# A hybrid SSD/GLA layer on one core: the first block's sums of squares taken from the columns of x by TensorE, columns in eight buffers, the first unit's split weights stored in block two

## The chip, the cores and the metric

The kernel runs on one core of one Trainium2 chip. The metric is device time in microseconds (us) of one execution. A core has five engines that run their own instruction streams and wait for each other by semaphores: PE (TensorE, matrix products; its weight loads are listed apart as PEld), DVE (VectorE), ACT (ScalarE), POOL (GpSimd) and SP (SyncE, which here only issues DMA transfers). "DVEq", "SPq" and so on are the instruction queues of the engines. Data lives in the chip's main memory (HBM) and is brought by DMA into the on-chip buffer (SBUF); PE writes its results into accumulation banks (PSUM).

## The reference

One layer of a decoder. 16 learned "meta" tokens are put in front of 2048 tokens of width 1024; each token is normalised by its root mean square; one combined projection gives the inputs of two branches and their gates:

```python
h = concatenate([meta_tokens, x], axis=1)              # (1, 2064, 1024)
u = h * rsqrt(mean(h * h, axis=-1) + EPS) * norm_w     # rmsnorm
proj = einsum('bld,dn->bln', u, w_in)
z, xbc, dt_raw, q, k, v, g_gla, a_lr, merge_g = split_cols(proj, IN_WIDTHS)
...
branches = stack([y_ssd, y_gla], axis=2)
merged = sum(sigmoid(merge_g) * einsum('blnc,ncd->blnd', branches, w_branch), axis=2)
out = rmsnorm(h + einsum('bld,de->ble', merged, w_out))[:, N_META:]
```

`y_ssd` comes from a causal convolution and a Mamba-2 scan, `y_gla` from gated linear attention; both carry a state from chunk to chunk. The change touches only how u is formed for the first tokens, and when some split weights are stored.

## The kernel before, in words

**Blocks and units.** The 2048 tokens are worked on in four blocks of 512 (four chunks of 128); the first block has the 16 meta tokens in front, 528 columns in all. In each block eight units run in a fixed order: four of the SSD branch (`ssd_proj`, i = 0 to 3) and four of the GLA branch (`gla_proj`). A unit projects u with its weights on PE; the scans that follow are generators, of which `step()` runs a piece at each `yield` of the unit. For PE and SP the order of the program is the order of execution (`manual_schedule`); on the other engines, and for the start ahead of the blocks, a scheduler orders by program order among what is ready in its own simulation. After the four blocks a second part computes gates, branch products and output.

**Split precision.** u and the weights are split in two parts each, hi = rounded to the matrix format by ACT, lo = value - hi; a product is three matmuls (`accum`, L176 to L179: hi x hi at L177, hi x lo at L178, lo x hi at L179).

**Weights.** `load_w` (L155) gives a split weight tile. The first time a key is seen, in block one, it loads the raw tile into one of three `wr` buffers (L163), ACT copies it to hi (L164), POOL subtracts to lo (L165) into one of four `whl` buffers, and the pair is put on a list to be stored in HBM as `k_...`; `save(n)` (L170 to L173) issues those stores on SP until n are left, and is called with 2 before each raw load and with 0 at the end of each block. In the later blocks a tile comes back already split, by one DMA (L159). The very first unit has the key `zm`: eight tiles of 128 x 288 (one for each 128 rows of the weight), used in pairs; for each pair four chunks of 128 tokens, and in block one the meta tokens, are multiplied (`proj_tok`). It yields once, before its third pair.

**The side job.** In block two, from unit 0 on, `beside_unit` forms sums of pieces of `w_out`: `make_sums` takes two of the three `wr` buffers, loads four pieces on SP (L76), subtracts on POOL (L80), and stores by the ACT queue (L83). It takes its first step at the yield in the middle of unit zm.

**u for a block.** `load_u(b)` (L229): for each chunk the rows of x are read, ACT squares and sums them (L241), and r = (mean + eps)^-0.5 follows on DVE and POOL (L250, L251). PE spreads r over the partitions by a matmul with the identity (L264, L268). Then for each of eight column tiles `xk` (128 features x 528 tokens, from `xmt`, the transposed x) DVE multiplies by norm_w and r (L280), ACT makes uh (L282), the ACT queue stores the tile as `u_left` (L283), and DVE makes ul (L284). `xk` uses the tag `acc`, which has two buffers. For the first block all of it runs ahead of the first unit; for the others it runs beside unit 4 of the block before.

Of the kernel before, what the change touches and what calls it, by code (L numbers as in the profile page):

```python
# [19 lines left out]
NCH = BLK // P  # L20
# [3 lines left out]
EPS = 1e-6  # L24
NWR = 3
NSQ = 5
NT4 = 5
NACT = 8
# [12 lines left out]
def trunk_kernel(ctx: ExitStack, tc: tile.TileContext, xm, xmt, w_feat, w_tok, w_zm, w_br, w_o,  # L41
                 cf32, cmsk, pvec, fnw, hvec, gw2, out):
    nc = tc.nc
# [5 lines left out]
    def mk(pool, shape, dt, tag, **kw):  # L49
        cnt[0] += 1  # L50
        return pool.tile(shape, dt, tag=tag, name=f"{tag}_{cnt[0]}", **kw)

    base = ctx.enter_context(tc.tile_pool(name="base", bufs=1))
    wdram = ctx.enter_context(tc.tile_pool(name="wdram", bufs=1, space=bass.MemoryType.DRAM))
    dpool = ctx.enter_context(tc.tile_pool(name="dpool", bufs=2, space=bass.MemoryType.DRAM))
    mhalf = base.tile([P, 4], F32, name="mhalf")
# [3 lines left out]
    def left(name):  # L60
        return wdram.tile([P, BLK], F32, tag=name, name=name, bufs=1)

    u_left = [[left(f"u_{b}_{kt}") for kt in range(KT)] for b in range(nblk)]
# [40 lines left out]
    for s in range(nsb):  # L104
        b = 2 * s + 2
# [9 lines left out]
    upool = first.enter_context(tc.tile_pool(name="upool", bufs=2))  # L115
    wpool = first.enter_context(tc.tile_pool(name="wpool", bufs=3))
    bpool = first.enter_context(tc.tile_pool(name="bpool", bufs=1))
    wk = first.enter_context(tc.tile_pool(name="wk", bufs=2))
    sm = first.enter_context(tc.tile_pool(name="sm", bufs=4))
    const = first.enter_context(tc.tile_pool(name="const", bufs=1))  # L120
    pj = first.enter_context(tc.tile_pool(name="pj", bufs=3, space=bass.MemoryType.PSUM))
    pt = first.enter_context(tc.tile_pool(name="pt", bufs=3, space=bass.MemoryType.PSUM))
    pc = first.enter_context(tc.tile_pool(name="pc", bufs=2, space=bass.MemoryType.PSUM))

    def bank(pool, tag):
        return mk(pool, [P, 512], F32, tag)


    cst = const.tile([P, 4, P], F32, name="cst")
    ident = cst[:, 0, :]  # L130
    tri = cst[:, 1, :]
    tris = cst[:, 2:4, :]
    pv = const.tile([P, 118], F32, name="pv")
    norm_w = pv[:, 0:8]
# [7 lines left out]
    ones = ones_r.bitcast(F32)  # L142
# [9 lines left out]

    kept, unsaved = {}, []

    def load_w(key, src):  # L155
        n = src.shape[-1]
        hl = mk(wpool, [P, 2, 512], F32R, "whl", bufs=4)[:, :, :n]
        if key in kept:
            nc.sync.dma_start(hl.bitcast(F32), kept[key])  # L159
        else:  # L160
            save(2)
            raw = mk(wpool, [P, 512], F32, "wr", bufs=NWR)[:, :n]
            nc.sync.dma_start(raw, src)  # L163
            nc.scalar.activation(hl[:, 0], raw, AF.Copy)  # L164
            nc.gpsimd.tensor_tensor(hl[:, 1], raw, hl[:, 0].bitcast(F32), op=ALU.subtract)  # L165
            kept[key] = wdram.tile([P, 2, n], F32, tag="k_" + key, name="k_" + key, bufs=1)
            unsaved.append((kept[key], hl.bitcast(F32)))
        return hl[:, 0], hl[:, 1]

    def save(n):  # L170

        while len(unsaved) > n:
            nc.sync.dma_start(*unsaved.pop(0))  # L173
# [7 lines left out]
    def proj_feat(key, src, segs, moving):  # L181

        pss = [bank(pj, "pj") for _ in segs]
        for half in range(2):
            h, lo = load_w(f"{key}_{half}", src[:, half * 512:(half + 1) * 512])
            for k4 in range(4):
                kt = half * 4 + k4
                cs = slice(k4 * P, (k4 + 1) * P)
                for ps, (a, n) in zip(pss, segs):
                    accum(ps[:, :n], (h[:, cs], lo[:, cs]), moving(kt, a, n), kt == 0, kt == KT - 1)  # L190
        return pss

    def proj_tok(key, src, u, starts, banks, width=256, per=2, sub=None):

        nq = KT // per
        opened = set()
        for q0 in range(0, nq, 2):
            if q0 == nq // 2:  # L200
                yield
            ws = [load_w(f"{key}_{q}", src[:, q * per * width:(q + 1) * per * width]) for q in (q0, q0 + 1)]
            for i, ((bk, ps), a) in enumerate(zip(banks, starts)):
                c0 = sub if sub is not None and i >= NCH else 0
                for k2 in range(2 * per):
                    kt = q0 * per + k2
                    h, lo = ws[k2 // per]
                    cs = slice(k2 % per * width + c0, (k2 % per + 1) * width)
                    accum(ps[:, c0:width], tuple(t[:, kt, a:a + P] for t in u),
                          (h[:, cs], lo[:, cs]), bk not in opened, kt == KT - 1, skip_group_check=True)  # L210
                    opened.add(bk)
# [14 lines left out]
        nc.vector.tensor_tensor(lo, src, h.bitcast(F32), op=ALU.subtract)  # L226


    def load_u(b):  # L229
        m0 = META if b == 0 else 0  # L230
        row0 = META - m0 + b * BLK
        tt = m0 + BLK
        pair = mk(upool, [P, 2, KT * (META + BLK)], F32R, "u")[:, :, :KT * tt]
        uh, ul = [pair[:, i].rearrange("p (k t) -> p k t", k=KT) for i in range(2)]

        def rows_rstd(r0, n):
            ss = mk(sm, [P, 1], F32, "ss")
            if m0:
                xt = mk(wk, [P, D], F32, "tok4", bufs=NT4)
                nc.sync.dma_start(xt[:n], xm[r0:r0 + n, :])  # L240
                nc.scalar.activation(xt[:n], xt[:n], AF.Square, accum_out=ss[:n])  # L241
            else:
                s2 = mk(sm, [P, 2], F32, "ss2")
                for i in range(2):
                    xt = mk(wk, [P, META + BLK], F32, "acc")[:, :BLK]
                    nc.sync.dma_start(xt, xm[r0:r0 + n, i * BLK:(i + 1) * BLK])
                    nc.scalar.activation(xt, xt, AF.Square, accum_out=s2[:, i:i + 1])
                nc.vector.tensor_tensor(ss, s2[:, 0:1], s2[:, 1:2], op=ALU.add)
            r = mk(sm, [P, 1], F32, "rs1")
            nc.vector.tensor_scalar(r[:n], ss[:n], 1.0 / D, EPS, op0=ALU.mult, op1=ALU.add)  # L250
            nc.gpsimd.tensor_tensor(r[:n], r[:n], mhalf[:n, 0:1], op=ALU.pow)  # L251
            return r

        rs = []
        for c in range(NCH):
            rs.append(rows_rstd(META + b * BLK + c * P, P))
            yield
        if m0:
            rs.append(rows_rstd(0, META))
            nc.sync.dma_start(cst[:, :2], cf32[:, :2])  # L260
            nc.sync.dma_start(pv, pvec)
        rb = bank(pt, "pt")
        for c in range(NCH):
            nc.tensor.matmul(rb[:, c * P:(c + 1) * P], rs[c].to_broadcast([P, P]), ident, start=True, stop=True)  # L264
        rbs = [(rb, m0, BLK)]
        if m0:
            rm = bank(pt, "pt")
            nc.tensor.matmul(rm[:, :META], rs[NCH][:META].to_broadcast([META, P]), ident[:META, :META],  # L268
                             start=True, stop=True)
            rbs = [(rm, 0, META)] + rbs  # L270
        else:
            rbc = mk(wk, [P, 3 + META + BLK], F32, "cin")[:, :BLK]
            nc.scalar.activation(rbc, rb, AF.Copy)
            rbs = [(rbc, 0, BLK)]
            yield
        for kt in range(KT):
            xk = mk(wk, [P, META + BLK], F32, "acc")[:, :tt]
            nc.sync.dma_start(xk, xmt[:, kt, row0:row0 + tt])
            for ps, a, n in rbs:
                nc.vector.scalar_tensor_tensor(xk[:, a:a + n], xk[:, a:a + n], norm_w[:, kt:kt + 1], ps[:, :n],  # L280
                                               op0=ALU.mult, op1=ALU.mult)
            nc.scalar.activation(uh[:, kt, :tt], xk, AF.Copy)  # L282
            nc.scalar.dma_start(u_left[b][kt], xk[:, m0:])  # L283
            nc.vector.tensor_tensor(ul[:, kt, :tt], xk, uh[:, kt, :tt].bitcast(F32), op=ALU.subtract)  # L284
            yield
        return uh, ul

    next_u = {}

    def fetch_u(b):  # L290
        next_u[b] = yield from load_u(b)

    for _ in fetch_u(0):
        pass


    nc.sync.dma_start(cst[:, 2:], cf32[:, 2:])
    hv = const.tile([P, 2, NH], F32, name="hv")
# [11 lines left out]
    nc.scalar.activation(nega, hv[:, 1], AF.Exp)  # L310
    nc.vector.tensor_scalar(nega, nega, -1.0, None, op0=ALU.mult)

    w2r = mk(wk, [P, META + BLK], F32, "act", bufs=NACT)[:48, :512]
    for i in range(3):
        nc.sync.dma_start(w2r[16 * i:16 * i + 16, :], gw2)
    w2 = const.tile([48, 512], F32R, name="w2")
# [700 lines left out]
    for si, st in enumerate(stages):  # L1017
        for q in range(28):
            p, j = PS[q // 4], q % 4
# [5 lines left out]
    i = 14  # L1025
# [102 lines left out]
```

## Time and profile before

| what | value |
|---|---|
| three runs | 2385.71, 2382.58, 2387.70 us |
| their median | 2385.71 us |
| profiled execution: span from the first to the last instruction | 2382.4 us |
| mean granted TensorE clock in it | 0.976 |
| bytes moved by DMA | 518.07 MB, 217 GB/s over the span |
| busy PE, DVE, ACT, POOL | 95%, 66%, 50%, 29% |

The profile is of one execution; its span is the time from the first to the last instruction, and the time of a run has a little around it. A group's row reads: line, engine, operation, tiles written <- read, shapes, count | busy us, mean ns of one | idle time of the engine just before, and what released it. A row of the timeline reads: start us, length us, engine, line, operation, tiles, count [idle before <- releaser]. "PEclk" is the clock that was granted to TensorE, as a share of the full one.

### The profile page before, as it was taken

To read this page: it belongs to the slowest core of one execution; us is meant where nothing else is said; L and a number is where in the kernel's file an instruction comes from. 1 tells how busy PE (TensorE), PEld (TensorE's weight loads), DVE (VectorE), ACT (ScalarE), POOL (GpSimd) and SP (SyncE) were. 2 spreads that over 40 slices of the span, in tenths; PEclk is the share of its full clock that TensorE was granted. 3 is DMA by queue.
4 is the path that set the end of the run, shared out by engine and by line. 5 is a ranking of instruction groups with operands and counts; after the bars stand their busy time and mean duration, and the time that the engine had idled before them with its cause. 6 is when DMAs were issued, how large, how long until landed. Compare 5 with 4: busy or idle time off the path is not lost. (4 is left out here: it accounts for less than half of the span.)

```text
span 2382.4 us, 36669 instructions
## 1 busy us (share of the span) xinstructions
PE 2264.0 (95%) x12641; PEld 1970.8 (83%) x12641; DVE 1571.8 (66%) x2889; ACT 1187.5 (50%) x2764; POOL 680.0 (29%) x681
## 2 busy tenths in 40 slices
PE   6899999999999999999999999789989999998998
PEld 6889989888889988888989889668877788877786
DVE  4676665676675676676666655764757855786976
ACT  4665655465544455544455534364634445553443
POOL 3343433122222122321122100324433454332431
PEclk8999999999999999999999999789999999999999
DMA  8665875667786676786666654364777965787652
GB/s 271 213 209 193 293 240 190 225 201 235 245 276 184 215 220 220 258 267 199 208 213 212 205 167 143 131 217 136 263 248 264 313 198 173 251 264 225 231 177 106
DMA packets 301547, 518.07 MB, mean 217 GB/s; under 512 B 27696, under 2 KB 143664, under 8 KB 301360
## 3 DMA queue, kind: packets, MB, share of 16 engines
q1 hardware_dynamic: 231856, 452.66, 58.2%
q10 hardware_dynamic: 69504, 63.06, 8.0%
q8 instruction: 99, 1.62, 0.3%
q14 instruction: 88, 0.72, 0.1%
HBM read 368.42 MB, written 147.19 MB: 216 GB/s over the span
## 5 line engine op out<-in xcount | busy, mean ns | idle before, releaser
L177 PE MATMUL pj<-u,whl 128*128 128x512 f32 (+1 forms) x1184 | 447.4, 378 | 9.3 <-ACT g_all L420 3.3
L179 PE MATMUL pj<-u,whl 128*128 128x512 f32 (+1 forms) x1184 | 431.5, 364 | 0.8 <-POOL whl L165 0.8
L178 PE MATMUL pj<-u,whl 128*128 128x512 f32 (+1 forms) x1184 | 430.9, 364 | 0.0
L177 PE MATMUL pj<-whl,u 128*128 128x256 f32 (+1 forms) x992 | 289.9, 292 | 8.7 <-ACT u L282 6.1
L179 PE MATMUL pj<-whl,u 128*128 128x256 f32 (+1 forms) x992 | 284.1, 286 | 1.3 <-DVE u L284 1.3
L177 PE MATMUL psa<-b,a 128*128 128x512 f32 x640 | 255.5, 404 | 30.8 <-ACT sn L913 20.6
L178 PE MATMUL pj<-whl,u 128*128 128x256 f32 (+1 forms) x992 | 283.8, 286 | 0.7 <-POOL whl L165 0.5
L177 PEld LDWEIGHTS pj<-u,whl 128*128 128x128 f32 x1184 | 225.7, 191 | 47.1 <-ACT g_all L420 3.7
L179 PE MATMUL psa<-b,a 128*128 128x512 f32 x640 | 255.8, 400 | 2.3 <-DVE a L897 2.2
L179 PEld LDWEIGHTS pj<-u,whl 128*128 128x128 f32 x1184 | 225.2, 190 | 36.7 <-POOL whl L165 1.1
L178 PE MATMUL psa<-b,a 128*128 128x512 f32 x640 | 255.5, 399 | 0.0
L178 PEld LDWEIGHTS pj<-u,whl 128*128 128x128 f32 x1184 | 225.8, 191 | 33.2
L876 DVE TENSOR_TENSOR b<-br,b 128x512 fp32r<-128x512 f32 x196 | 160.8, 842 | 59.3 <-ACT b L875 58.9
L177 PEld LDWEIGHTS pj<-whl,u 128*128 128x128 f32 x992 | 191.0, 193 | 9.7 <-ACT u L282 6.6
L179 PEld LDWEIGHTS pj<-whl,u 128*128 128x128 f32 x992 | 191.2, 193 | 2.1 <-DVE u L284 2.1
L178 PEld LDWEIGHTS pj<-whl,u 128*128 128x128 f32 x992 | 191.1, 193 | 2.0 <-POOL whl L165 1.6
L897 DVE TENSOR_TENSOR a<-ar,a 128x512 fp32r<-128x512 f32 x160 | 136.2, 855 | 83.1 <-ACT a L896 82.6
L80 POOL TENSOR_TENSOR wr<-wr 128x256 f32<-128x256 f32 x80 | 66.2, 828 | 430.9 <-DMA wr<-y 173.0
L165 POOL TENSOR_TENSOR whl<-wr,whl 128x512 fp32r<-128x512 f32 (+1 forms) x100 | 132.7, 1334 | 191.6 <-ACT whl L164 166.3
L875 ACT ACTIVATE b<-br 128x512 fp32r<-128x512 f32 x196 | 119.8, 627 | 133.4 <-DMA br<-br_t 35.4
L177 PEld LDWEIGHTS psa<-b,a 128*128 128x128 f32 x640 | 124.9, 195 | 61.8 <-ACT sn L913 24.1
L462 DVE SCALAR_TENSOR_TENSOR acc<-cin,hcw,acc 128x512 f32<-128x512 f32 (+1 forms) x192 | 156.3, 814 | 26.8 <-ACT acc L458 26.1
(267 smaller groups left out, 5025.1 us busy)
## 6 DMA issues: line engine op xcount, KB each, us to landing
whl<-k_s SPq DMA_DIRECT2D x96, 512.0 KB, 4.5
whl<-k_g SPq DMA_DIRECT2D x96, 512.0 KB, 4.2
whl<-k_v SPq DMA_DIRECT2D x48, 512.0 KB, 3.9
whl<-k_z SPq DMA_DIRECT2D x36, 512.0 KB, 3.7
wr<-in_w_feat SPq DMA_DIRECT2D x64, 256.0 KB, 4.4
k_s<-whl SPq DMA_DIRECT2D x32, 512.0 KB, 3.5
cb<-cumd ACTq DMA_DIRECT2D x64, 256.0 KB, 5.7
y<-gg ACTq DMA_DIRECT2D x64, 256.0 KB, 4.6
```

The costliest lines, as they stand in the source:

```text
L80: nc.gpsimd.tensor_tensor(o, x, y, op=ALU.subtract)
L165: nc.gpsimd.tensor_tensor(hl[:, 1], raw, hl[:, 0].bitcast(F32), op=ALU.subtract)
L177: nc.tensor.matmul(ps, sh, mh, start=first, stop=False, **kw)
L178: nc.tensor.matmul(ps, sh, ml, start=False, stop=False, **kw)
L179: nc.tensor.matmul(ps, sl, mh, start=False, stop=last, **kw)
L462: nc.vector.scalar_tensor_tensor(acc, cin[:, k:k + tt], hcw[:, ti, k:k + 1], acc, op0=ALU.mult, op1=ALU.add)
L875: nc.scalar.activation(t[:, 0], raw, AF.Copy)
L876: nc.vector.tensor_tensor(t[:, 1], raw, t[:, 0].bitcast(F32), op=ALU.subtract)
L897: nc.vector.tensor_tensor(t[:, 1], src, t[:, 0].bitcast(F32), op=ALU.subtract)
```

## The change

Three things are changed. The first block gets its u from a new function `first_u`: all eight column tiles are loaded into the eight `act` buffers; ACT (even tiles) and DVE (odd tiles) square them into `tok4` buffers; PE sums the squares over the features with the squares as weights and two columns of ones as the moving operand, five groups of 128 tokens (the meta group overlaps the first chunk), accumulating over the eight tiles in one bank; r is formed for all five at once; and the rest is as before, moved into `to_u`. No rows of x are read for block one. `load_u` is left with the case of the later blocks. Second, `load_w` does not store the `zm` tiles when they are seen first: in block two they are loaded raw and split a second time, and stored then; and a load of a kept tile now also issues one pending store ahead of itself. Third, the staging of `gw2` moves from `act` to `acc`.

```diff
+    seen = set()
     def load_w(key, src):
         ...
         if key in kept:
+            save(max(0, len(unsaved) - 1))
             nc.sync.dma_start(hl.bitcast(F32), kept[key])
         else:
             save(2)
             ...
-            kept[key] = wdram.tile([P, 2, n], F32, tag="k_" + key, name="k_" + key, bufs=1)
-            unsaved.append((kept[key], hl.bitcast(F32)))
+            if key.startswith("zm") and key not in seen:
+                seen.add(key)
+            else:
+                kept[key] = wdram.tile([P, 2, n], F32, tag="k_" + key, name="k_" + key, bufs=1)
+                unsaved.append((kept[key], hl.bitcast(F32)))
...
+    def to_u(b, kt, xk, rbs, m0, uh, ul):
+        for ps, a, n in rbs:
+            nc.vector.scalar_tensor_tensor(xk[:, a:a + n], xk[:, a:a + n], norm_w[:, kt:kt + 1], ps[:, :n],
+                                           op0=ALU.mult, op1=ALU.mult)
+        nc.scalar.activation(uh[:, kt, :m0 + BLK], xk, AF.Copy)
+        nc.scalar.dma_start(u_left[b][kt], xk[:, m0:])
+        nc.vector.tensor_tensor(ul[:, kt, :m0 + BLK], xk, uh[:, kt, :m0 + BLK].bitcast(F32), op=ALU.subtract)
+
+    def first_u():
+        tt = META + BLK
+        uh, ul = u_pair(tt)
+        xs = []
+        for kt in range(KT):
+            xs.append(mk(wk, [P, META + BLK], F32, "act", bufs=NACT))
+            nc.sync.dma_start(xs[kt], xmt[:, kt, :tt])
+            if kt == 3:
+                nc.sync.dma_start(cst[:, :2], cf32[:, :2])
+                nc.sync.dma_start(pv, pvec)
+        at = [0] + [META + c * P for c in range(NCH)]
+        sums_ps = bank(pt, "pt")
+        sq = [mk(wk, [P, 2, META + BLK], F32, "tok4", bufs=NT4) for _ in range(KT // 2)]
+        for kt in range(KT):
+            t = sq[kt // 2][:, kt % 2]
+            if kt % 2:
+                nc.vector.tensor_tensor(t, xs[kt], xs[kt], op=ALU.mult)
+            else:
+                nc.scalar.activation(t, xs[kt], AF.Square)
+            for i, a in enumerate(at):
+                nc.tensor.matmul(sums_ps[:, 2 * i:2 * i + 2], t[:, a:a + P], ones[:, :2],
+                                 start=kt == 0 and i == 0, stop=kt == KT - 1, skip_group_check=True)
+        n = len(at)
+        r = mk(sm, [P, 5], F32, "rs5", bufs=1)
+        nc.vector.tensor_scalar(r, sums_ps[:, :2 * n].rearrange("p (i two) -> p i two", two=2)[:, :, 0], 1.0 / D, EPS,
+                                op0=ALU.mult, op1=ALU.add)
+        nc.gpsimd.tensor_tensor(r, r, mhalf[:, 0:1].to_broadcast([P, n]), op=ALU.pow)
+        rb, rm = bank(pt, "pt"), bank(pt, "pt")
+        for c in range(NCH):
+            nc.tensor.matmul(rb[:, c * P:(c + 1) * P], r[:, c + 1:c + 2].to_broadcast([P, P]), ident,
+                             start=True, stop=True)
+        nc.tensor.matmul(rm[:, :META], r[:META, 0:1].to_broadcast([META, P]), ident[:META, :META],
+                         start=True, stop=True)
+        for kt in range(KT):
+            to_u(0, kt, xs[kt], [(rm, 0, META), (rb, META, BLK)], META, uh, ul)
+        return uh, ul
...
-    for _ in fetch_u(0):
-        pass
+    next_u[0] = first_u()
...
-    w2r = mk(wk, [P, META + BLK], F32, "act", bufs=NACT)[:48, :512]
+    w2r = mk(wk, [P, META + BLK], F32, "acc")[:48, :512]
```

More of the change, by code (lines that the diff above doesn't have):

```diff
@@ L226, in split, with u_pair @@
         nc.vector.tensor_tensor(lo, src, h.bitcast(F32), op=ALU.subtract)
-    def load_u(b):
[L230 to L234, printed above, removed]
+    def u_pair(tt):
+        pair = mk(upool, [P, 2, KT * (META + BLK)], F32R, "u")[:, :, :KT * tt]
+        return [pair[:, i].rearrange("p (k t) -> p k t", k=KT) for i in range(2)]
@@ L236, in rows_rstd @@
+    def load_u(b):
+        row0 = META + b * BLK
+        uh, ul = u_pair(BLK)
         def rows_rstd(r0, n):
             ss = mk(sm, [P, 1], F32, "ss")
[L238 to L248, printed above, removed]
+            s2 = mk(sm, [P, 2], F32, "ss2")
+            for i in range(2):
+                xt = mk(wk, [P, META + BLK], F32, "acc")[:, :BLK]
+                nc.sync.dma_start(xt, xm[r0:r0 + n, i * BLK:(i + 1) * BLK])
+                nc.scalar.activation(xt, xt, AF.Square, accum_out=s2[:, i:i + 1])
+            nc.vector.tensor_tensor(ss, s2[:, 0:1], s2[:, 1:2], op=ALU.add)
@@ L255, in load_u @@
         for c in range(NCH):
[L256 removed]
+            rs.append(rows_rstd(row0 + c * P, P))
             yield
[L258 to L261, printed above, removed]
         rb = bank(pt, "pt")
@@ L264, in load_u @@
             nc.tensor.matmul(rb[:, c * P:(c + 1) * P], rs[c].to_broadcast([P, P]), ident, start=True, stop=True)
[L265 to L275, printed above, removed]
-        for kt in range(KT):
[L277 to L284, printed above, removed]
+        rbc = mk(wk, [P, 3 + META + BLK], F32, "cin")[:, :BLK]
+        nc.scalar.activation(rbc, rb, AF.Copy)
+        yield
+        for kt in range(KT):
+            xk = mk(wk, [P, META + BLK], F32, "acc")[:, :BLK]
+            nc.sync.dma_start(xk, xmt[:, kt, row0:row0 + BLK])
+            to_u(b, kt, xk, [(rbc, 0, BLK)], 0, uh, ul)
             yield
```

## The prediction

> **What bounds the kernel now.** First I read the page's busy shares.
>
> ```profile
> PE 2264.0 (95%) x12641; PEld 1970.8 (83%) x12641; DVE 1571.8 (66%) x2889; ACT 1187.5 (50%) x2764; POOL 680.0 (29%) x681
> ```
>
> TensorE (PE) is the bound, so a gain has to come out of its 118 us of idleness or out of time at a low clock. Next come the stretches around the change, seven at the start and two in block two. Columns: stretch, length, busy us (and count) of PE, weight loads, DVE, ACT, POOL, then granted clock, DMA share, GB/s.
>
> ```profile
> 0.00:15.50 15.50, 2.70 (x10) 2.33 (x10) 4.71 (x20) 9.79 (x20) 2.95 (x9) 1.00 0.85 282
> 15.50:22.27 6.77, 6.12 (x30) 5.45 (x30) 4.48 (x8) 2.44 (x5) 3.03 (x4) 1.00 0.78 240
> 22.27:26.64 4.37, 4.29 (x32) 3.95 (x31) 0.17 (x1) 0.89 (x2) 1.99 (x3) 1.00 1.01 341
> 26.64:32.10 5.46, 1.13 (x3) 0.57 (x4) 2.50 (x6) 2.16 (x4) 1.84 (x3) 0.86 1.03 344
> 32.10:38.28 6.18, 6.18 (x27) 5.78 (x27) 0.75 (x1) 0.25 (x1) 0.19 (x1) 0.57 0.89 285
> 38.28:48.07 9.79, 6.74 (x31) 6.50 (x31) 5.42 (x13) 4.14 (x11) 2.51 (x2) 0.65 0.61 216
> 48.07:60.00 11.93, 11.93 (x99) 11.82 (x99) 6.54 (x15) 8.93 (x21) 5.83 (x6) 1.00 0.69 250
> 430.20:436.60 6.40, 6.40 (x51) 6.40 (x50) 4.06 (x11) 2.21 (x6) 1.47 (x2) 1.00 0.69 196
> 438.90:445.40 6.50, 6.50 (x50) 6.47 (x49) 1.65 (x6) 2.70 (x11) 0.00 (x0) 1.00 0.74 256
> ```
>
> The first projection unit ("zm", eight weight tiles used in four pairs) runs from 15.5 to 48.07. A pair has 30 matmuls: 4.4 us in 22.27:26.64, and 6.2 us at a clock of 0.57 in 32.10:38.28. From 48.07 PE is full. In block two the same unit (430.2 to 436.6 and 438.9 to 445.4, the gap between filled by a scan) leaves no idle time. Why the first one is slow, by the waits of PE, DVE and SP up to 48 us (total, times, longest) and SP's timeline:
>
> ```profile
> PE pj L177 <- ACT u L282: 6.1, 3, 3.2
> DVE acc L280 <- DMA acc<-in_xmt: 13.7, 3, 5.8
> SPq L278 <- DMA u<-acc: 5.3, 4, 3.9
> SPq L173 <- POOL whl L165: 9.6, 8, 4.4
> ...
> 16.45 1.04 SPq L278 DMA_DIRECT2D acc<-in_xmt  x2
> 24.11 0.34 SPq L278 DMA_DIRECT2D acc<-in_xmt  x1
> 25.85 0.55 SPq L278 DMA_DIRECT2D acc<-in_xmt  x1
> 33.62 1.91 SPq L278 DMA_DIRECT2D acc<-in_xmt  x2
> ```
>
> The columns of x go through two buffers. Columns 2 and 3 are asked for at 16.45, the last two at 33.62: each waits until a buffer has been normalised, split and stored, and stands on SP behind weight stores (L173) that wait for POOL. PE waits for columns.
>
> **The change: the start.** The four row tiles and the meta rows are not read (2.1 MB), the eight zm stores (8 x 288 KB) leave the start, and all columns are requested at once. The rows that give the prices:
>
> ```profile
> 4.88 1.06 ACT L241 ACTIVATE tok<-tok 128x1024 f32<-128x1024 f32 x1 [2.35 <-DMA tok<-in_xm]
> 10.10 0.20 DVE L302 TENSOR_SCALAR hcw<-pv 128x64 f32<-128x64 f32 x1 [1.33 <-DMA pv<-in_pvec]
> 10.00 1.83 PEld L264 LDWEIGHTS pt<-cst,rs 128*128 128x128 f32 x8 [10.00 <-POOL rs L251]
> 11.31 0.18 ACT L241 ACTIVATION_READ_ACCUMULATOR tok<-tok 16x1 f32 x1
> 12.35 0.61 PE L268 MATMUL pt<-cst,rs 16*128 16x16 f32 x2 [0.22 <-POOL rs L251]
> 15.54 0.61 PE L177 MATMUL pj<-whl,u 128*128 128x288 f32 x1 [2.58 <-ACT whl L164]
> 20.39 0.29 PE L179 MATMUL pj<-whl,u 128*128 128x288 f32 x1
> k_zm<-whl SPq DMA_DIRECT2D x8, 288.0 KB, 4.0
> 99.56 0.53 PEld L547 LDWEIGHTS pc<-c,sq 128*128 128x128 f32 x4
> L280 DVE SCALAR_TENSOR_TENSOR acc<-acc,pv,pt 128x512 f32<-128x512 f32 (+1 forms) x16 | 6.9, 485 | 14.2 <-DMA acc<-in_xmt 13.7 <-PE pt L264 0.5
> L284 DVE TENSOR_TENSOR u<-acc,u 128x528 fp32r<-128x528 f32 x8 | 7.0, 896 | 1.5 <-ACT u L282 1.4
> L282 ACT ACTIVATE u<-acc 128x528 fp32r<-128x528 f32 x8 | 5.0, 642 | 5.6 <-DVE acc L280 4.7 <-DMA wr<-in_w_zm 0.8
> ```
>
> 1. Landing. Before, the same bytes (four row tiles, meta rows, two constants) were in by 10.1 (the DVE row that waits for pv). So the last column is in by about 10.1, the first near 4.2 (half a row tile; a whole one was used at 4.88).
> 2. Squares: 0.64 on ACT, about 0.7 on DVE, alternating, so faster than landing: hidden. PE starts near 4.9.
> 3. Sums on TensorE: 8 columns x 5 groups = 40 fp32 matmuls. L264 shows two weight loads for each fp32 matmul (8 for its 4), so 80 loads of 128x128, each moving two columns. The step is 0.23 at the start (1.83 us for 8) and 0.11 once warm (L547: 4 in 0.53, the last 0.19 being its own length). The first burst of zm started at 15.54 with 0.61 and had shortened to 0.29 by 20.39, so it was cold for some 4.6 us; with that, 21 loads by 9.5 and 59 x 0.113 = 6.7 us more: 16.2. From below, if PE keeps up with the landing, 10.1 + 0.7 + 10 x 0.113 = 11.9; from above, if the clock never rises, 4.9 + 80 x 0.22 = 22.5. I take 16.2, because every dense burst in the rows above did warm up.
> 4. r: from the last read (11.49) to PE's use (12.35) it took 0.86; with the drain, 17.3. Ten weight loads to spread it over the partitions (1.83 + 0.61 = 2.4 us cold, 1.1 warm), I take 1.7: 19.0.
> 5. DVE per column 6.9/8 + 0.71 (the usual length of L284; one of the eight was longer) = 1.6, so a pair every 3.2 us; the first pair is split at about 21.4, the last at 31.8. ACT's 0.64 hides beside it.
> 6. PE: one pair at the low clock, 6.2, then three at 3.8 (4.4 less its waits), 17.6: zm ends at 39.0. From 48.07 that is a **gain of 9.1**; 11.5 if the first pair is at full clock too (36.6), 2.8 if step 3 stays cold.
>
> The Trainium skill, page "TensorE: Matmul & The Clock Gate", section on LDWEIGHTS, gives 128 columns over 1.2 GHz, an estimate of 107 ns a load, without a second price for a cold array. L547 agrees, L264's 0.23 does not. By the page the sums would end at 13.5 and the gain be 2.7 us more; the rows decide.
>
> What costs nothing: the three gw2 loads move to the acc buffers, which nobody else uses before the convolution that follows zm; if that cover went, SP would wait a buffer's round, 24.11 - 16.45 = 7.7 us. The columns sit in all eight act buffers, which the next stage wants after 39, when they are stored. The squares take four tok buffers, the mask staging the fifth; zm's outputs want them only at its end. The work that follows (48.07:60.00, PE full) is paced by its own chain and moves up with zm's end.
>
> **The change: block two.** The zm weights now come raw: per tile a 144 KB load into one of three wr buffers, an ACT copy, a POOL subtraction, a 288 KB store on SP; before, one 288 KB load. That is 8 more copies and subtractions and 2.4 MB of stores, beside matmuls of 12.9 us. The catch is wr: in the middle of the unit the side job that forms sums of w_out (L76, L80) takes two of the three wr buffers.
>
> ```profile
> L164 ACT ACTIVATE whl<-wr 128x288 fp32r<-128x288 f32 x8 | 3.4, 440 | 6.8 <-DMA wr<-in_w_zm 6.8
> L165 POOL TENSOR_TENSOR whl<-wr,whl 128x288 fp32r<-128x288 f32 x8 | 7.1, 891 | 12.9 <-ACT whl L164 12.9
> wr<-in_w_zm SPq DMA_DIRECT2D x8, 144.0 KB, 3.9
> out_t<-wr ACTq DMA_DIRECT2D x4, 256.0 KB, 3.9
> 420.82 10.03 SPq L159 DMA_DIRECT2D whl<-k_zm  x4
> 416.32 2.64 POOL L165 TENSOR_TENSOR whl<-wr,whl 128x512 fp32r<-128x512 f32 x2 [6.43 <-PE pt L179]
> 430.94 1.98 SPq L76 DMA_DIRECT2D wr<-in_w_o  x4
> 434.98 0.73 POOL L80 TENSOR_TENSOR wr<-wr 128x256 f32<-128x256 f32 x1 [16.02 <-DMA wr<-in_w_o]
> 437.42 0.73 POOL L80 TENSOR_TENSOR wr<-wr 128x256 f32<-128x256 f32 x1
> ```
>
> One pass through a wr buffer is 3.9 (load) + 0.44 + 0.85 (a little under L165's mean) = 5.2 us. In times of before: the last wr buffers of block one return at 418.96 (L165), so tiles 0 to 2 load from 419.4; the four whl buffers come free between 420.8 and 430.9 (the spread of the four L159 loads), so tile 3, in the first wr to return, is split at 432.5, in time. The side job takes the other two wr near 426 and 429 and, done as before (POOL to about 437, a store of 3.9), gives them back at about 438.5 and 441. Tile 4 gets tile 3's buffer: ready 438.5, just in time for 438.9. Tile 5 is asked for at 438.5 and split at 443.5, but wanted at 439.3: **a stall of 4.3 us**. Tiles 6 and 7 come at about 444 and 446.3, wanted from 446.4: in time. Behind the wait on SP stand the next unit's loads, due 4 us later too, and three zm stores; ACT and POOL have slack (2.70 and 0 busy in 438.90:445.40). From below the stall is 0, if the buffers return four microseconds sooner; from above 11.5, below.
>
> The clock may fall after such a gap: the 5.46 us of 26.64:32.10, with three matmuls in it, were followed by 0.57, and a pair then costs 6.2 - 3.8 = 2.4 us more. The stall is shorter than that stretch, so I leave the 2.4 out of the sum and keep it for the range. By the Trainium skill, same page, Part 1 (the HAM clock gate), about 3.4 us of idleness throttle the array again, a rule against this change; by it the sum below would be 2.4 us worse.
>
> **Sum.** -9.1 + 4.3 = -4.8 on the span of 2382.4, that is 2377.6. The three runs have a median of 2385.7, 3.3 above that span, so I forecast 2380.9. About 0.2%, 4.8 us, is what a measurement can tell from no change.
>
> **Rivals.**
> - *No stall in block two.* The scheduler may hand the side job its buffers later, or POOL free them sooner; for it: POOL idle 16 us before 434.98. Against: the side job's loads stand ahead of tile 4's in SP's order. 2385.7 - 9.1 = 2376.6.
> - *One wr buffer for the whole second half* (slower). If the side job keeps both until the unit is over, tiles 4 to 7 pass singly, 5.2 us each: split at 438.5, 443.7, 448.9, 454.1, the unit ends near 456.8 instead of 445.4, +11.4, net +2.3: 2388.0, and 2390.4 with a low-clock pair. It decides once the stall passes 9.1 us. For it: the side job's store waits on ACT's queue behind other work. Against: before, it was through with POOL 7 us after its loads.
> - *Sums that stay cold.* Two moving columns a load may be too little work to raise the clock, and PE becomes the start's bound: sums until 22.5, gain 2.8, net +1.5: 2387.2. For it: no row shows a burst so thin. Against: the short L547 loads ran warm.
>
> **How the numbers follow.** Forecast 0.42 (own range 2378.5 to 2383.3: the 11.5 of step 6, and the 2.4 of a cold pair); no stall 0.26; one buffer 0.16; cold sums 0.16. Faster than 2380.9: half of the forecast, all of "no stall" and 0.01 of mixtures, 0.48; slower than 2390.5: half of "one buffer" and 0.06 where cold sums meet a cold restart in block two, 0.14; the rest, 0.38, is the same. For 8 in 10 the range runs from 2374 (no stall with step 6's better end) to 2390.
>
> **What would show it.** Right: 80 thin matmuls from about 5 to 16, with steps falling to 0.11; the last zm matmul near 39; no rows of x read in block one; in block two an idle PE of 3 to 5 us inside zm, released by whl after a load into wr. Wrong: steps of 0.22 throughout the sums; zm ending after 45 or before 36; no idle in block two's zm, or one above 9 us; a wait that is new between 60 and 420, which I have priced at nothing.

## The result, and the profile after

The changed kernel takes 2394.09 us (median of 17 runs, 2389.01 to 2399.79), the kernel before beside it 2382.58 (17 runs, 2376.71 to 2391.49): a ratio of 1.0039, 95% interval 1.0027 to 1.0050. It is **slower**, by 11.5 us between the medians and by 9.3 by the ratio (6.4 to 11.9), where I had forecast 4.8 us less, and 2394.09 lies above the range.

The page of the changed kernel, busy shares:

```profile
PE 2283.2 (95%) x12721; PEld 1990.2 (83%) x12721; DVE 1582.6 (66%) x2889; ACT 1188.3 (50%) x2766; POOL 695.5 (29%) x685
```

TensorE runs 80 instructions more, those of the sums, and is busy 19.2 us longer. The span is 2398.0, 15.6 more than before; this execution, 2399.79 us, was the longest of the 17, so a few us of the 15.6 are its own. The timeline of the start (start us, length, engine, line, operation, tiles, count, idle time before and what ended it; L183 to L185 are the old L177 to L179, L167 and L168 the old L164 and L165, and L241, L243, L244, L245 the old L280, L282, L283, L284):

```profile
4.28 17.23 PE L267 MATMUL pt<-ones_r,tok 128*128 128x2 f32 x80 [4.28 <-ACT tok L265]
...
10.59 0.71 DVE L263 TENSOR_TENSOR tok<-act 128x528 f32<-128x528 f32 x1 [0.93 <-DMA act<-in_xmt]
...
21.79 1.18 POOL L273 TENSOR_TENSOR rs<-rs,mhalf 128x5 f32<-128x5 f32 x1 [3.51 <-DVE rs L271]
23.02 2.07 PE L276 MATMUL pt<-cst,rs 128*128 128x128 f32 x8 [1.51 <-POOL rs L273]
25.02 0.60 PE L278 MATMUL pt<-cst,rs 16*128 16x16 f32 x2
25.13 6.49 DVE L241 SCALAR_TENSOR_TENSOR act<-act,pv,pt 128x512 f32<-128x512 f32 x16 [3.42 <-PE pt L276]
25.91 2.30 ACTq L244 DMA_DIRECT2D u<-act  x4
28.26 1.18 ACT L243 ACTIVATE u<-act 128x528 fp32r<-128x528 f32 x2 [10.85 <-DVE act L241]
...
31.54 5.03 DVE L245 TENSOR_TENSOR u<-act,u 128x528 fp32r<-128x528 f32 x8
...
32.29 0.61 PE L185 MATMUL pj<-whl,u 128*128 128x288 f32 x1 [2.49 <-DVE u L245]
...
49.90 0.37 PE L183 MATMUL pj<-u,whl 128*128 128x264 f32 x1
```

The columns are in and squared by about 11, but the 80 loads run one after the other until 21.5. Then DVE does all sixteen multiplications (L241) before the first subtraction (L245, 31.54), and ACT's queue issues four stores of u (L244) ahead of its first copy (28.26). PE has all that it needs only from 32.29; the next unit's first matmul, which ends zm, starts at 49.90, against 48.07 before and the 39.0 of the forecast.

That is 1.8 us of the loss. To see the rest I matched the same instruction in both profiles. Its start in the run less its start before is called the **shift** below. It is given at times of the kernel before, and from matmuls; for instance, these two rows of ACT, of before and of after, show the same +11.0 near the end of block one as the matmuls:

```profile
375.25 0.60 ACT L616 ACTIVATE gg<-pj 128x512 f32<-128x512 f32 x1 [1.57 <-PE pj L179]
```

```profile
386.29 0.60 ACT L644 ACTIVATE gg<-pj 128x512 f32<-128x512 f32 x1 [1.57 <-PE pj L185]
```

The shift is +1.8 at the end of zm, +2.4 at 62, +6.0 at 90, +7 at 238, +11.0 at 430, +13.9 at 461 (behind zm of block two) and +16.1 at 654; from there it goes up and down between 12 and 18 and is +15.8 near the end. So three places lose: the start missed its gain, block one lost 9.2, block two 2.9 and a little behind it. Block one from the end of zm to the first zm matmul of block two, and two stretches of it, first before, then after (columns as in the prediction: the granted clock is third from the end):

```profile
48.07:430.27 382.20, 362.35 (x2564) 337.42 (x2564) 252.51 (x480) 222.26 (x567) 147.08 (x132) 0.97 0.65 222
...
50.00:90.00 40.00, 38.08 (x311) 36.93 (x309) 24.94 (x38) 25.49 (x62) 18.01 (x17) 1.00 0.80 274
...
300.00:430.00 130.00, 125.73 (x836) 113.84 (x837) 82.31 (x164) 62.99 (x160) 44.30 (x33) 1.00 0.63 215
```

```profile
49.90:441.28 391.38, 369.40 (x2564) 344.27 (x2564) 251.10 (x477) 223.30 (x570) 150.05 (x135) 0.95 0.66 221
...
50.00:90.00 40.00, 37.29 (x293) 36.42 (x293) 20.19 (x31) 22.27 (x53) 16.52 (x16) 0.96 0.82 264
...
300.00:430.00 130.00, 124.61 (x832) 114.35 (x831) 77.11 (x148) 66.15 (x168) 46.21 (x34) 0.96 0.62 211
```

The 2564 matmuls are the same. They take 7.1 us longer (369.40 for 362.35) at a granted clock of 0.95 instead of 0.97, and PE is idle for 2.1 us more: most of the 9.2 us is time at a low clock. In the two stretches the clock is lower by 0.04. What comes ahead of the first fall is seen in the timelines of ACT and PE, of before and of after (L164 and L167 split the next unit's weights, 128 x 512; the store of `cumd` and ACT's wait for its landing belong to the unit's decay sums):

```profile
38.03 1.15 ACT L164 ACTIVATE whl<-wr 128x512 fp32r<-128x512 f32 x2 [5.99 <-DMA acc<-in_xmt]
...
51.37 0.61 ACT L164 ACTIVATE whl<-wr 128x512 fp32r<-128x512 f32 x1
...
65.24 0.20 ACT L455 ACTIVATE cin<-tails 128x3 f32<-128x3 f32 x1 [0.33 <-DMA cumd<-cin]
```

```profile
45.95 1.15 ACT L167 ACTIVATE whl<-wr 128x512 fp32r<-128x512 f32 x2 [3.06 <-PE pc L185]
...
53.08 0.63 ACT L167 ACTIVATE whl<-wr 128x512 fp32r<-128x512 f32 x1 [1.84 <-DMA wr<-in_w_feat]
56.17 0.63 ACT L167 ACTIVATE whl<-wr 128x512 fp32r<-128x512 f32 x1 [0.88 <-DMA wr<-in_w_feat]
...
69.41 0.20 ACT L483 ACTIVATE cin<-tails 128x3 f32<-128x3 f32 x1 [2.06 <-DMA cumd<-cin]
...
72.42 0.59 PE L183 MATMUL pj<-u,whl 128*128 128x264 f32 x1 [2.49 <-ACT acc L486]
```

Before, zm's last pair waited for columns, and the next unit's first two tiles were split at 38.03, ten us ahead of their use at 48.07. After, zm runs densely, they are split at 45.95, four us ahead of 49.90, and then ACT stands waiting for raw weights, 1.84 and 0.88 us. Then ACT waits 2.06 us for a store of `cumd` to land, where it had waited 0.33. Just ahead of 72.42 PE is idle for 2.49 us, released by ACT (0.3 before, at the same line of the program), and the first matmul after that takes 0.59, against 0.37 at 49.90. So it is not the weights that this gap of PE waits for, but for the most part a store that lands late. What holds it up is not shown; the DMA share is 0.92 from 65.5 to 69.4, and was 0.64 from 63.1 to 65.2 before.

In block two, the first and last matmul of zm before and after, with POOL and SP beside it:

```profile
430.27 0.38 PE L177 MATMUL pj<-whl,u 128*128 128x288 f32 x1
...
445.28 0.29 PE L179 MATMUL pt<-whl,u 128*128 128x288 f32 x1
```

```profile
441.28 0.38 PE L183 MATMUL pj<-whl,u 128*128 128x288 f32 x1
...
443.78 0.80 POOL L80 TENSOR_TENSOR wr<-wr,wr 128x256 f32<-128x256 f32 x1
444.55 1.25 POOL L168 TENSOR_TENSOR whl<-wr,whl 128x288 fp32r<-128x288 f32 x1
...
445.82 0.33 SPq L166 DMA_DIRECT2D wr<-in_w_zm  x1
...
455.37 0.40 PE L184 MATMUL pj<-whl,u 128*128 128x288 f32 x1 [0.47 <-POOL whl L168]
...
457.98 0.30 PE L185 MATMUL pt<-whl,u 128*128 128x288 f32 x1
```

From first to last it takes 16.7 us instead of 15.0. The splitting of a tile (L168) stands on POOL behind the side job (L80), the next raw load waits on SP for the buffer (445.82), and PE waits 0.47 for a split. That is the queue for the `wr` buffers that I had predicted, but not its stall of 4.3: in zm PE is idle for only 0.8 us, and the rest of the 1.7 is matmuls that take longer. Another 1.2 us is lost just behind zm.

### The profile page after: what moved, and what is told of

Its sections match the earlier page's. It is cut to its first block, busy times and chain, and to the rows that moved or that the text cites. A ratio compares the mean times of both kernels' runs of the same rounds, so it can differ in the third digit from the quotient of the medians.

```text
span 2398.0 us, 36832 instructions
## 1 busy us (share of the span) xinstructions
PE 2283.2 (95%) x12721; PEld 1990.2 (83%) x12721; DVE 1582.6 (66%) x2889; ACT 1188.3 (50%) x2766; POOL 695.5 (29%) x685
## 3 DMA queue, kind: packets, MB, share of 16 engines
q8 instruction: 100, 1.64, 0.3%
## 5 line engine op out<-in xcount | busy, mean ns | idle before, releaser
L183 PE MATMUL pj<-u,whl 128*128 128x512 f32 (+1 forms) x1184 | 449.8, 380 | 13.3 <-DMA whl<-k_g 3.7
L185 PE MATMUL pj<-u,whl 128*128 128x512 f32 (+1 forms) x1184 | 433.6, 366 | 0.8 <-POOL whl L168 0.8
L183 PE MATMUL pj<-whl,u 128*128 128x256 f32 (+1 forms) x992 | 290.1, 292 | 3.6 <-ACT u L243 3.3
L183 PE MATMUL psa<-b,a 128*128 128x512 f32 x640 | 253.6, 401 | 35.2 <-ACT sn L941 21.6
L185 PE MATMUL pj<-whl,u 128*128 128x256 f32 (+1 forms) x992 | 283.5, 286 | 2.5 <-DVE u L245 2.5
L183 PEld LDWEIGHTS pj<-u,whl 128*128 128x128 f32 x1184 | 227.7, 192 | 51.7 <-DMA whl<-k_g 4.5
L185 PEld LDWEIGHTS pj<-u,whl 128*128 128x128 f32 x1184 | 227.0, 192 | 36.8 <-POOL whl L168 1.1
L185 PE MATMUL psa<-b,a 128*128 128x512 f32 x640 | 254.4, 397 | 1.3 <-DVE a L925 1.2
L168 POOL TENSOR_TENSOR whl<-wr,whl 128x512 fp32r<-128x512 f32 (+1 forms) x108 | 139.6, 1301 | 221.0 <-ACT whl L167 183.3
L183 PEld LDWEIGHTS pj<-whl,u 128*128 128x128 f32 x992 | 191.2, 193 | 4.4 <-ACT u L243 3.4
L185 PEld LDWEIGHTS pj<-whl,u 128*128 128x128 f32 x992 | 191.0, 193 | 2.8 <-DVE u L245 2.8
L80 POOL TENSOR_TENSOR wr<-wr 128x256 f32<-128x256 f32 x80 | 69.6, 870 | 393.8 <-DMA wr<-y 170.7
L183 PEld LDWEIGHTS psa<-b,a 128*128 128x128 f32 x640 | 123.6, 193 | 67.0 <-ACT sn L941 25.6
```

What stands on the lines that cost most here:

```text
L80: nc.gpsimd.tensor_tensor(o, x, y, op=ALU.subtract)
L183: nc.tensor.matmul(ps, sh, mh, start=first, stop=False, **kw)
L185: nc.tensor.matmul(ps, sl, mh, start=False, stop=last, **kw)
```

## The experiments

Twelve kernels, each timed beside the kernel before, whose own median was between 2382.58 and 2384.89 us. All medians, with zm's end and the shifts of the profiled run:

| run | median us (runs) | ratio to before, 95% | zm ends | shift at 430 | at 461 |
|---|---|---|---|---|---|
| the changed kernel | 2394.09 (17) | 1.0039 [1.0027, 1.0050] | 49.90 | +11.0 | +13.9 |
| e1: zm stored in block one | 2394.77 (6) | 1.0042 [1.0026, 1.0058] | 49.16 | +10.4 | +10.4 |
| e2: before, zm stored in block two | 2383.49 (12) | 0.9987 [0.9973, 1.0001] | 42.22 | -2.4 | +0.6 |
| e3: before, columns in eight buffers | 2380.47 (12) | 0.9982 [0.9966, 0.9998] | 41.04 | -5.0 | -5.0 |
| e4: one-pass sums | 2382.33 (12) | 0.9986 [0.9972, 1.0000] | 42.26 | -1.7 | +0.8 |
| e5: 96 columns of ones | 2390.13 (12) | 1.0025 [1.0010, 1.0040] | 43.89 | +3.7 | +6.9 |
| e6: e4, ordered | 2385.39 (12) | 1.0000 [0.9986, 1.0014] | 39.95 | -2.6 | +1.0 |
| e7: e3, ordered | 2375.90 (12) | 0.9971 [0.9951, 0.9992] | 42.77 | -8.3 | -8.2 |
| e8: e2 and e3 together | 2379.78 (12) | 0.9983 [0.9969, 0.9996] | 40.73 | -8.9 | -6.6 |
| e9: changed kernel, ordered | 2392.09 (12) | 1.0032 [1.0017, 1.0048] | 46.69 | +7.2 | +10.4 |
| e10: e1 and e4 together | 2381.92 (12) | 0.9993 [0.9976, 1.0010] | 42.36 | -0.7 | -0.5 |
| e11: e10, last pair twice | 2385.25 (12) | 1.0013 [0.9996, 1.0031] | 46.19 | -0.3 | -0.3 |
| e12: changed kernel, last pair twice | 2390.89 (12) | 1.0024 [1.0009, 1.0038] | 52.81 | +5.4 | +7.6 |

A shift is of one execution and carries a few us of its own; totals are judged by the ratios.

**Block two, or the start?** e1 takes the storing of zm back to block one.

```diff
-            if key.startswith("zm") and key not in seen:
-                seen.add(key)
-            else:
-                kept[key] = ...
-                unsaved.append(...)
+            kept[key] = ...
+            unsaved.append(...)
```

> The changed kernel, but the split zm tiles are stored in block one again. Theory A (the thin sums at the start are the main loss, block two a small one): the sums still take 17 us, zm still ends near 50 to 52, and block two gives back some 3 us: about 2390, +7 over before. Theory B (splitting zm a second time in block two is the main loss): at most 2385, within 3 of before. Theory C (mostly chance of which windows have the clock halved): about as the changed kernel, +9 to +12.

The total stayed at 2394.77, so block two is not where most of the loss is. But its own price shows: between 430 and 461 the shift does not move.

e2 is the converse, the same storing put into the kernel before (its diff is the one above, turned round, with the save ahead of a kept load):

> The kernel before with nothing but the zm tiles stored in block two (loaded raw and split twice). A: the start loses eight stores from SP's queue and zm ends 1 to 3 us sooner, block two loses about 3: +0 to +3 over before. B: +8 or more. C: within 3 of before.

Here zm ends 5.9 us sooner, with the stores out of SP's queue, and nothing of that is left at 461. The total is not the 0 to 3 above before that I had expected, but the same as before within its interval.

**The buffers alone.** e3 reads the rows as before and only gives the columns of block one eight buffers (the staging of `gw2` moves to `acc` with it, as in the change; not shown):

```diff
-            xk = mk(wk, [P, META + BLK], F32, "acc")[:, :tt]
+            xk = (mk(wk, [P, META + BLK], F32, "act", bufs=NACT) if m0
+                  else mk(wk, [P, META + BLK], F32, "acc"))[:, :tt]
```

> The kernel before with nothing but the columns of the first block in eight buffers: rows of x are still read and summed by ACT, zm still stored in block one. A: r is ready at 12 as before, first pair of zm split near 19, then 17.6 us of matmuls: zm ends near 38 instead of 48, total -4 to -9 (some of the ten is given back because the next unit's weights are no longer split ahead of time). B: as A at the start. A rival to both, that the lead in weights is all that counts after zm: zm ends near 38 but the total is within 2 of before.

zm ends at 41.04, 7.0 sooner than before, with the rows read and no sums on TensorE: the buffers alone bring most of the 9.1 that I had forecast for the whole.

**The sums.** e4 makes the squares and the ones fp32r, so that each product needs one load instead of two:

```diff
-        sq = [mk(wk, [P, 2, META + BLK], F32, "tok4", bufs=NT4) ...]
+        sq = [mk(wk, [P, 2, META + BLK], F32R, "tok4", bufs=NT4) ...]
...
-                nc.tensor.matmul(sums_ps[...], t[:, a:a + P], ones[:, :2],
+                nc.tensor.matmul(sums_ps[...], t[:, a:a + P], ones_r[:, :2],
```

> The changed kernel with the squares rounded to the matrix format, so that each sum matmul is one pass: 40 loads instead of 80 (the sums of squares are rounded a little more coarsely). A: the sums take half, 8.6 us or what the landing allows, about 13 instead of 21.5; zm ends near 42 instead of 50; total 8 below the changed kernel, about +3 over before. B: the start is earlier but the total falls by less than 3, because the loss lies in block two. If thin loads have another price in this format, the step between loads will show it.

Its timeline:

```profile
4.26 8.69 PE L267 MATMUL pt<-ones_r,tok 128*128 128x2 f32 x40 [4.26 <-ACT tok L265]
```

40 loads in 8.69 us, the same 0.217 each; zm ends 7.6 us sooner than in the changed kernel and the total is 11.8 lower. The two intervals lie apart: the cold fp32 sums are the largest single cost that an experiment took away. Why they stay at 0.215 each is asked by e5, which keeps fp32 and moves 96 columns of ones instead of two:

```diff
-                nc.tensor.matmul(sums_ps[:, 2 * i:2 * i + 2], t[:, a:a + P], ones[:, :2],
+                nc.tensor.matmul(sums_ps[:, 96 * i:96 * i + 96], t[:, a:a + P], ones[:, :96],
```

> The changed kernel with 96 columns of ones under each load of the sums instead of 2: more work for TensorE, same 80 loads, same result. Theory A1 (the clock stays halved because two moving columns a load do not count as work): the steps fall from 0.215 to about 0.11 after one or two windows of 3.4 us, the sums end near 14 to 16 instead of 21.5, zm ends near 43, total 5 to 8 below the changed kernel (about 2387). Theory A2 (a load of fp32 weights at the start costs 0.215 at any clock, or the landing holds it): the sums end at 21.5 or later, total as the changed kernel or above, 2394 to 2397.

The timeline of e5, and then the same stretches of the start, of the changed kernel and of e5:

```profile
4.23 11.84 PE L267 MATMUL pt<-ones_r,tok 128*128 128x96 f32 x80 [4.23 <-ACT tok L265]
19.09 1.18 PE L276 MATMUL pt<-cst,rs 128*128 128x128 f32 x8 [3.02 <-POOL rs L273]
```

```profile
4.00:9.00 5.00, 4.72 (x23) 4.72 (x23) 1.79 (x7) 1.51 (x3) 0.00 (x0) 1.00 0.99 333
9.00:14.00 5.00, 5.00 (x25) 5.00 (x25) 2.85 (x5) 2.06 (x5) 0.05 (x1) 1.00 0.80 240
14.00:21.50 7.50, 7.50 (x36) 7.42 (x35) 0.00 (x0) 1.08 (x3) 3.04 (x4) 1.00 0.30 79
```

```profile
4.00:9.00 5.00, 4.77 (x22) 4.77 (x23) 2.46 (x7) 1.51 (x4) 0.00 (x0) 1.00 1.03 349
9.00:14.00 5.00, 5.00 (x43) 5.00 (x43) 2.19 (x4) 2.37 (x6) 0.40 (x1) 1.00 0.69 216
...
20.00:30.00 10.00, 4.18 (x17) 3.58 (x16) 9.69 (x22) 4.81 (x8) 0.00 (x0) 0.50 0.57 211
```

With two columns a load starts every 5.00 / 25 = 0.20 us from 9 to 14 and every 7.50 / 36 = 0.21 from 14 to 21.5: no change. With 96, the step falls from 0.22 to 5.00 / 43 = 0.116 between 9 and 14, and the same number of loads is over after 11.84 us instead of 17.23. More work, faster: two moving columns did not raise the clock here. The total is lower by only 4.0, less than the 6.0 that zm's end gained, and its interval overlaps the changed kernel's; the shift grew again, from -4.2 at zm's end to +3.7 at 430.

**The order on DVE and ACT.** e6 (on e4), e7 (on e3) and e9 (on the changed kernel) write the order by hand: column by column, the subtraction of a column one step behind its multiplication, the stores of u after all copies.

```diff
+        with tc.manual_schedule(engines={mybir.EngineType.DVE, mybir.EngineType.Activation}):
+            for kt in range(KT + 1):
+                if kt < KT:
+                    for ps, a, n in [(rm, 0, META), (rb, META, BLK)]:
+                        nc.vector.scalar_tensor_tensor(xs[kt][:, a:a + n], ...)
+                    nc.scalar.activation(uh[:, kt], xs[kt], AF.Copy)
+                if kt:
+                    nc.vector.tensor_tensor(ul[:, kt - 1], xs[kt - 1], uh[:, kt - 1]..., op=ALU.subtract)
+            for kt in range(KT):
+                nc.scalar.dma_start(u_left[0][kt], xs[kt][:, META:])
```

> The one-pass sums, and after r the first block's normalising and splitting in a fixed order on DVE and ACT: multiply tile k, split tile k - 1, and the eight stores of u after all copies. If the order (all eight multiplications ahead of the first subtraction, four stores ahead of the first copy) costs what the changed kernel's trace shows, the first pair is split near 21.5 instead of 25.6, zm ends near 38.5 instead of 42.4, total 2 to 4 below the one-pass kernel without it. Rival: zm ends sooner but the total stays within 1.5, because block one then waits for the next unit's weights.

> Rows of x summed by ACT as before, columns in eight buffers, the fixed order on DVE and ACT, zm stored in block one. r is ready at 12.5, the first pair split near 16, the weights split among them by 18: zm ends near 36 instead of 41; total 2 to 4 below the eight-buffer kernel without the order, that is 2376 to 2379. Rival as in the run beside it: total within 1.5 of that kernel.

> The changed kernel with its fp32 sums, and only the order on VectorE and ScalarE set at the start: column by column, the stores of u behind all copies. Theory A (the sums, not the order, are the main loss): the sums still take 17.2 us and end at 21.5; the first pair is split near 31 (as long after the end of the sums as with one-pass sums in order, 9.5 us), zm ends near 48 to 48.5 instead of 49.9, and the total stays within 2 us of the changed kernel's: 2391 to 2395. Rival (the order that the scheduler chose is worth the 4.3 us that my step 5 missed by): zm ends near 45.6 and the total is near 2388 to 2390.

e6 ends zm at 39.95, 2.3 sooner than e4, and its total shows no gain by it. e9 ends it at 46.69, between the two expectations; its timeline shows the columns coming evenly:

```profile
28.59 0.70 DVE L288 TENSOR_TENSOR u<-act,u 128x528 fp32r<-128x528 f32 x1
...
30.01 0.70 DVE L288 TENSOR_TENSOR u<-act,u 128x528 fp32r<-128x528 f32 x1
```

1.42 us a column. The order is worth 49.90 - 46.69 = 3.2 us of zm's end, and its total is inside the changed kernel's interval. e7 did not end zm at 36: PE waits for its first weights until 18.79, and from there zm takes 24.0 us instead of about 18. The split of later weights stands on ACT behind the eight stores of u, which this order had put at the end, and PE waits for it once more:

```profile
18.79 0.61 PE L177 MATMUL pj<-whl,u 128*128 128x288 f32 x1 [6.02 <-ACT whl L164]
...
32.29 0.40 PE L177 MATMUL pj<-whl,u 128*128 128x288 f32 x1 [1.67 <-ACT whl L164]
```

```profile
26.61 5.09 ACTq L291 DMA_DIRECT2D u<-act  x8
31.80 1.11 ACT L164 ACTIVATE whl<-wr 128x288 fp32r<-128x288 f32 x3 [4.55 <-DMA u<-act]
```

Still it has the lowest median of all, 0.9971 [0.9951, 0.9992], below both kernels; its interval overlaps that of e3. It has a **later** end of zm than e3, and 3.3 us more of lead at 430.

**Do the parts add?** e8 is e2 and e3 together, the change without its sums on TensorE:

> Rows of x summed by ACT, columns in eight buffers, zm stored in block two: the change without the sums on TensorE. If the gains add, zm ends near 37 (no stores in SP's way), block two gives back 3 us, and the total is 4 to 8 below before. If both gains are the same wait of the start, seen twice, the total is that of the eight-buffer kernel or 2 above it (block two's price): -1 to -4 against before.

2379.78 is e3's time within the interval: the parts do not add. e10 has one-pass sums and zm stored in block one:

> The changed kernel with one-pass sums (40 loads) and zm stored in block one again, so block two is as before. If the storing in block two costs 2 to 4 us there and the eight stores are hidden at the start: zm ends near 42.4 as with one-pass sums alone, no step of the shift at 430 to 460, total 2378 to 2381. Rival (the eight stores get back into the way at the start, on SP ahead of other loads): zm ends 1 to 3 us later, the total is the same as with one-pass sums alone, 2381 to 2384.

Block two's step is gone (-0.7 to -0.5), the total is e4's within the interval. e2, e3, e4, e6, e8 and e10 end zm between 39.95 and 42.36, and their totals, 2379.8 to 2385.4, do not follow that order: the earliest has the highest. They differ by little more than their intervals.

**Is block one paced by zm's end?** e11 (on e10) and e12 (on the changed kernel) multiply zm's last pair twice in block one:

```diff
-                for k2 in range(2 * per):
+                twice = key == "zm" and len(starts) > NCH and q0 == nq - 2
+                for k2 in (2 * list(range(2 * per)) if twice else range(2 * per)):
```

> The run with one-pass sums and zm stored in block one, but in block one the last pair of zm is multiplied twice, 30 matmuls or 3.8 us more on TensorE (zm's results are off by that). It asks whether block one is paced by the weights that come next, or by zm's end. Theory L (a lead: with all columns there, zm runs densely and the next unit's weights have no time to be split ahead; what zm gains, block one waits for later): zm ends near 46.2 instead of 42.4, but the shift against the kernel before at 430 stays near the -0.7 of that run (up to +1), total 2380 to 2384. Rival (TensorE is the bound all along, the delay stays): the shift at 430 is near +3, total near 2386.

> The changed kernel with the same doubling of zm's last pair in block one (30 matmuls, 3.8 us; zm's results are off by that). Theory L: zm ends near 53.7 instead of 49.9, the shift at 430 stays near +11 (9 to 12), total within 2 us of 2394. Rival (the delay stays): the shift at 430 is near +15, total near 2398.

In e11 zm ends 3.8 us later and the shift at 430 is -0.3, against -0.7: by then the delay has vanished. Its total, 2385.25, is nearer to the rival's: the intervals of e10 and e11 overlap, and in the profile the shift of e11 goes from -0.3 at 461 to +5.4 at 654, behind what the edit touches, which I did not follow. On the total e11 decides nothing. In e12 it ends 2.9 later, and at 430 the shift is +5.4 instead of +11.0, less than even theory L had; the total, 2390.89, is no higher than the changed kernel's (the intervals overlap). Its profiled execution was the shortest of its 12, the changed kernel's the longest of its 17; but e9's, also among its shortest, grew by 8.6 from zm's end to 430, so this alone does not explain the 0.7 of e12. The timeline and two stretches of e12:

```profile
52.71 0.63 ACT L167 ACTIVATE whl<-wr 128x512 fp32r<-128x512 f32 x1 [0.57 <-PE pc L185]
...
70.28 0.20 ACT L484 ACTIVATE cin<-tails 128x3 f32<-128x3 f32 x1 [0.60 <-DMA cumd<-cin]
...
72.93 0.39 PE L183 MATMUL pj<-u,whl 128*128 128x264 f32 x1 [0.67 <-ACT acc L487]
```

```profile
50.00:90.00 40.00, 39.33 (x324) 38.76 (x324) 21.11 (x33) 23.42 (x55) 16.86 (x16) 1.00 0.78 268
300.00:430.00 130.00, 124.97 (x841) 113.94 (x841) 78.87 (x154) 65.81 (x167) 45.17 (x33) 0.99 0.64 219
```

The wait for the weights is gone (ACT is released by PE), ACT waits 0.60 for the store of `cumd` instead of 2.06, PE 0.67 instead of 2.49, and the clock is 1.00 and 0.99 where it was 0.96. So in these traces block one's end does not follow zm's end.

## Why the prediction was wrong, by its steps

- **Steps 1 and 2** hold: the last column was there to be squared at 10.59 (10.1 + 0.5), PE started at 4.28 (4.9).
- **Step 3 failed.** I took 16.2 for the end of the sums "because every dense burst in the rows above did warm up"; it was 21.5, near the upper bound I had named (22.5). The bursts of zm that warmed up moved 288 columns a load, these two. e5 shows that this is the difference: with 96 columns the step fell to 0.116. +5.3.
- **Step 4**: from the end of the sums to the last spreading matmul 25.62 - 21.5 = 4.1 instead of 2.8: POOL's power took 1.18, and the ten loads 2.6, no faster than the 2.4 of a cold start. +1.3.
- **Step 5** sized the parts well (1.42 us a column in e9 for my 1.6) but assumed an order that the code does not fix. The scheduler put all multiplications first, and PE's dense work began 32.29 - 25.62 = 6.7 us after the spreading instead of 2.4: +4.3, of which the order is 3.2 by e9; what the other 1.1 is stays open. By the step's own 3.2 us a pair, the first pair would be split at 19.0 + 3.2 = 22.2, not at 21.4.
- **Step 6** held: 49.90 - 32.29 = 17.6, as written. 5.3 + 1.3 + 4.3 = 10.9, which is 49.9 - 39.0.
- **Block two**: right in its place, not in its stall. The shift grows between 430 and 461 by 2.3 to 3.6 in the seven profiles with zm stored in block two and ordinary last pair (e8 and e6 the ends), and by 0.0 to 0.2 in the four with it stored in block one; I had 4.3. In the changed kernel 1.7 of its 2.9 lies inside zm, with 0.8 us of idleness instead of one wait of 4.3: that the sizes are near each other is in part luck. In my sum, tile 5 is split at 438.5 + 5.2 = 443.7, as the second rival has it, not at 443.5, and its upper bound of 11.5 is the rival's 11.4; neither matters here.
- **"The work that follows ... moves up with zm's end" failed**, and with it the price of nothing for 60 to 420. In all seven profiles with sums on TensorE and an ordinary last pair the shift grew from zm's end to 430, by 4.1 to 9.3 us (in the changed kernel from +1.8 to +11.0); where the rows are read it grew by 3.5 (e2) and 2.0 (e3) and shrank in e7 and e8. e11 and e12 show that 3 to 4 us more in zm are gone by 430. Part of it can be placed. In the four profiles with fp32 sums and an ordinary last pair, and in no other, ACT waits 2.06 to 2.74 us for the store of `cumd` (at most 1.06 in the others), and PE is idle for 2.47 to 2.98 at the row shown at 72.42 (at most 1.06); from 62 to 90 their shift grows by 3.5 to 5.4, that of the nine others by at most 0.8. This is most of what fp32 sums lose more (7.9 to 9.3) than one-pass sums (4.1 to 5.5). ACT's wait for raw weights does not tell the two kinds apart: it stands in e4 (1.04) and e6 (1.64) too. Why the store lands late behind fp32 sums, and what takes the other 3 to 6 us, stays open; in the changed kernel it comes with a lower clock again (from 300 on).

The rival of cold sums had the mechanism of step 3, but put the change at +1.5 where 11.5 was measured: it kept steps 4 and 5 and the free block one.

## What to carry to other kernels

Before a reduction is moved to TensorE, count its weight loads and ask how many columns each moves: here, with two, all of them went at the cold price, however dense. A start that ends sooner is worth only what the work behind it can use; a delay put in at that point (e11, e12) shows in the trace whether it is. And where a sum reckons with two engines taking turns, see whether the program fixes their order: here it did not, and that moved zm's end by 2 to 3 us (e6, e9).

## What the runs showed of the hardware

Two moving columns a load did not raise the clock in 17.2 us of back-to-back work; 96 did between 5 and 10 us after the start. The eight spreading loads behind the sums say the same: 2.07 us after two columns (at 23.02), 1.18 after 96 (at 19.09). The Trainium skill, page "TensorE: Matmul & The Clock Gate", Part 1 (the HAM clock gate), says that what raises it is about 3.4 us of sustained activity, not a number of matmuls, and that everything issued after that runs at the full clock. The 96 columns agree roughly, the two columns do not: here the measurement decides.

The granted clock reads 1.00 in the stretches of the first 21.5 us of both, though the step halves inside one of them: at the start the length of a step tells the clock, not that column. After its sums, e5 read 0.50 from 20 to 30, once PE had been idle for 3.02 us waiting for r (its row at 19.09). In the changed kernel the idle 2.49 us ahead of 72.42 were followed by a matmul of 0.59, against 0.37 at 49.90.
